# A fixed plan of expert blocks without branches, with two blocks interleaved, in a decoder layer on one core

## The chip, the cores and the metric

The kernel runs on one core of a Trainium2 chip. The metric is the device time of one execution in microseconds (us); less is better. The engines of a core work side by side: PE (TensorE, matrix products and transposes), DVE (VectorE), ACT (ScalarE) and POOL (GpSimd); SP (SyncE) issues most of the transfers, which 16 DMA engines carry out. Each engine has a program of its own and waits for the others by semaphores.

## The reference

One decoder layer on 2048 tokens of 1024 channels in fp32: two token mixers side by side (differential attention, and a causal convolution module), a gated merge, then a mixture of 32 experts and a gated per-layer embedding. The change is in the experts:

```python
g_idx = argmax(t @ w_rg + b_rg)                       # one of 4 groups
top_p, top_e = top_k(softmax(e_logits[g_idx]), 2)     # two of its 8 experts
...
def expert_block(args):
    xb, e = args
    hdn = jax.nn.silu(xb @ w1[e]) * (xb @ w3[e])      # [rows, 1024] @ [1024, 512], twice
    return hdn @ w2[e]                                # [rows, 512] @ [512, 1024]
...
h = h + moe
ple_gate = sigmoid(rmsnorm(h) @ w_ple_gate + b_ple_gate)
h = h + ple_gate * (p @ w_ple_proj)
```

Each token goes to two experts, so 4096 rows are spread over 32 experts, unevenly, and how many rows each has is known at run time only.

## The kernel before

Every fp32 operand is split into two parts of type fp32r: `split` (L92, L93) lets ACT copy the high part and DVE or POOL subtract it from the whole for the low part. A product is then three products, high by high, high by low and low by high (`mm3`, L97 to L99, or the lines L1144 to L1147).

The stages follow each other: the mixers and the merge, the routing (`route`, `pick`), the experts (`moe`), the per-layer embedding (`ple`). `pick` sorts the experts: expert 0 comes first, the others are ranked by their number of rows, and heavy and light ones alternate. It writes `idx` and `dst` (the rows of each block of 128, for gathering and for scattering) and `slots` (for each place in the order: the expert, its number of rows, its number of blocks).

An expert has 12 weight units of 128 x 1024 (512 KB): eight of w1 and w3 side by side, four of w2. `pull` issues a unit's load on SP's queue into a raw buffer (`eraw`, 9 of them) and splits it into `ewh` and `ewl` (15 pairs); units 2, 6 and 10 of an expert have their low part made by POOL, the others by DVE. Where the pulls stand in the program is a table written by hand (`PULLS`). The order of all five engines in the loop is the order of the code.

A block of up to 128 rows is gathered by POOL (`xs`), transposed by PE and split (`turned`: `tps`, `xt`); for each half f of the 512 hidden columns PE makes 24 products of 512 columns into `ups`, ACT and DVE make silu(a) * b (`gated`: `hd`), PE turns it (`turn`: `hps`, split into `hh`), and the products with w2 go to `yd` (`down`), are copied to `y` and scattered by POOL. A full block has 72 products. A block of at most 64 rows ("few", `both`, L1130 to L1133) puts its high and low parts side by side and needs 48, and DVE adds the two halves of each sum (`total`, L1136, L1137).

An expert's first block is always a full one. After half f = 0 of it all five engines load the expert's number of rows (L976) and branch: over 128 rows (L1030) the second block is computed inside the branch, as a full one if there are more than 192 rows (L1034) and as a short one otherwise, with nothing of the next expert's weights in between; `many` has further branches for a third block (L1005, L1007, L1009, L1010). Behind the branch the first block goes on.

The first queue behind the experts is that of `ple`: projections of the embedding for the first tiles (`pps`, AHEAD of them in front), then each tile's two expert rows (`ys`, from the scattered `Y`), the norm (`hn`), its transposes and the gate's products (`gps`).

## Time and profile before

| | |
|---|---|
| time, median of 3 runs (lowest, highest) | 2960.14 us (2957.19, 2967.8) |
| profiled execution, span from first to last instruction | 2960.1 us |
| PE busy | 2736.7 us (92% of the span) |
| PE weight loads, beside the products | 2282.7 us (77%) |
| DVE busy | 2041.7 us (69%) |
| ACT busy | 1474.9 us (50%) |
| POOL busy | 722.3 us (24%) |
| HBM read, written | 424.66 MB, 102.50 MB |

The span of the profiled execution is its own time; the runs beside it are timed without a profile. Shares of busy time are averages over stages that have different limits. Durations of matmuls overlap: PE takes one of 512 columns every 0.23 us at full clock, though each is shown with 0.39, so prices are read from starts, not from durations.

### The profile page before, as it was taken

To read this page: it belongs to the slowest core of one execution; us is meant where nothing else is said; L and a number is where in the kernel's file an instruction comes from. 1 tells how busy PE (TensorE), PEld (TensorE's weight loads), DVE (VectorE), ACT (ScalarE), POOL (GpSimd) and SP (SyncE) were. 2 spreads that over 40 slices of the span, in tenths; PEclk is the share of its full clock that TensorE was granted. 3 is DMA by queue.
4 is the path that set the end of the run, shared out by engine and by line. 5 is a ranking of instruction groups with operands and counts; after the bars stand their busy time and mean duration, and the time that the engine had idled before them with its cause. 6 is when DMAs were issued, how large, how long until landed. Compare 5 with 4: busy or idle time off the path is not lost. (4 is left out here: it accounts for less than half of the span.)

```text
span 2960.1 us, 40065 instructions
## 1 busy us (share of the span) xinstructions
PE 2736.7 (92%) x14078; PEld 2282.7 (77%) x14078; DVE 2041.7 (69%) x2860; ACT 1474.9 (50%) x2712; POOL 722.3 (24%) x463
## 2 busy tenths in 40 slices
PE   7999999999999999999999989898888989888988
PEld 5888877997778788787898867676666767666776
DVE  6995249995878888657567456666667777776564
ACT  4233352335766667544444345555455656565443
POOL 2021130123111000001101134544335444452122
PEclk9999999999999999999999989999999999999999
DMA  5134443235243331456556366777767776876371
GB/s 189 60 107 142 159 147 104 93 114 196 81 132 89 104 112 53 160 184 214 168 170 206 122 238 243 265 287 259 252 223 274 276 283 236 293 274 244 125 246 56
DMA packets 180220, 531.52 MB, mean 180 GB/s; under 512 B 19185, under 2 KB 48641, under 8 KB 179361
## 3 DMA queue, kind: packets, MB, share of 16 engines
q1 hardware_dynamic: 135536, 397.02, 39.9%
q0 software_dynamic: 25904, 92.45, 8.5%
q10 hardware_dynamic: 18432, 37.76, 3.4%
q8 instruction: 177, 2.90, 0.4%
q14 instruction: 171, 1.39, 0.1%
HBM read 424.66 MB, written 102.50 MB: 178 GB/s over the span
## 5 line engine op out<-in xcount | busy, mean ns | idle before, releaser
L93 DVE TENSOR_TENSOR ewl<-eraw,ewh 128x1024 fp32r<-128x1024 f32 x365 | 597.2, 1665 | 94.4 <-ACT ewh L92 88.5
L92 ACT ACTIVATE ewh<-eraw 128x1024 fp32r<-128x1024 f32 x464 | 474.1, 1065 | 54.0 <-PE mps L98 24.9
L387 DVE SCALAR_TENSOR_TENSOR co<-cb,pvt,co 128x1024 f32<-128x1024 f32 x240 | 313.6, 1345 | 1.6
L93 POOL TENSOR_TENSOR ewl<-eraw,ewh 128x1024 fp32r<-128x1024 f32 x99 | 253.8, 2563 | 185.4 <-ACT ewh L92 183.0
L1146 PE MATMUL ups<-ewh,xt 128*128 128x512 f32 x592 | 250.0, 422 | 40.3 <-issue 38.6
L1147 PE MATMUL ups<-ewl,xt 128*128 128x512 f32 x592 | 244.5, 413 | 0.9 <-DVE ewl L93 0.5
L97 PE MATMUL ps<-uh,wh 128*128 128x512 f32 x576 | 232.0, 405 | 4.4 <-ACT uh L92 4.4
L586 DVE TENSOR_REDUCE nm<-sc 128x1 f32<-128x512 f32 (+3 forms) x320 | 185.3, 606 | 66.1 <-PE sc L583 51.6
L98 PE MATMUL ps<-ul,wh 128*128 128x512 f32 x576 | 227.9, 397 | 1.1 <-POOL ul L93 1.1
L99 PE MATMUL ps<-uh,wl 128*128 128x512 f32 x576 | 227.2, 396 | 0.0
L1146 PEld LDWEIGHTS ups<-ewh,xt 128*128 128x128 f32 x592 | 119.0, 201 | 71.9 <-issue 46.0
L97 PE MATMUL ps<-wh,uh 128*128 128x384 f32 x512 | 173.0, 338 | 0.0
L99 PE MATMUL ps<-wh,ul 128*128 128x384 f32 x512 | 172.1, 336 | 0.0
L98 PE MATMUL ps<-wl,uh 128*128 128x384 f32 x512 | 172.0, 336 | 0.0
L1144 PE MATMUL ups<-ewh,xt 128*128 128x512 f32 x592 | 167.5, 406 | 3.7 <-issue 3.7
L97 PE MATMUL mps<-ewh,mh 128*128 128x256 f32 x512 | 150.3, 294 | 4.1 <-ACT mh L92 4.1
L403 POOL DMA_DIRECT2D G<-sg x64 | 35.1, 549 | 457.3 <-ACT sg L402 325.2
L98 PE MATMUL mps<-ewl,mh 128*128 128x256 f32 x512 | 145.8, 285 | 0.0
L99 PE MATMUL mps<-ewh,ml 128*128 128x256 f32 x512 | 145.2, 285 | 0.0
L1147 PEld LDWEIGHTS ups<-ewl,xt 128*128 128x128 f32 x592 | 119.3, 202 | 25.5 <-DVE ewl L93 1.0
L430 POOL TENSOR_TENSOR qn<-qk,qk_std 128x1024 f32<-128x1024 f32 x16 | 44.6, 2785 | 380.7 <-DVE qk_std L189 363.8
L1204 POOL DMA_INDIRECT Y<-y,dst x48 | 72.3, 1507 | 266.3 <-POOLq L1034 188.3
(340 smaller groups left out, 7238.5 us busy)
## 6 DMA issues: line engine op xcount, KB each, us to landing
eraw<-in_we SPq DMA_DIRECT2D x384, 512.0 KB, 7.3
G<-sg POOLq DMA_DIRECT2D x64, 256.0 KB, 2.7
eraw<-in_wac SPq DMA_DIRECT2D x32, 512.0 KB, 4.3
ga<-G SPq DMA_DIRECT2D x32, 512.0 KB, 5.1
eraw<-in_wo SPq DMA_DIRECT2D x32, 512.0 KB, 3.7
ys<-Y SPq DMA_DIRECT2D x32, 512.0 KB, 8.2
wraw<-in_wqkv SPq DMA_DIRECT2D x16, 768.0 KB, 4.2
wraw<-in_wg SPq DMA_DIRECT2D x20, 512.0 KB, 3.9
```

Of the source, the lines that this page charges most:

```text
L92: nc.scalar.activation(hi, x, AF.Copy)
L93: (lo_eng or nc.vector).tensor_tensor(lo, x, f32(hi), ALU.subtract)
L97: nc.tensor.matmul(ps, lh, rh, start=start, stop=False)
L98: nc.tensor.matmul(ps, lh, rl, start=False, stop=False)
L99: nc.tensor.matmul(ps, ll, rh, start=False, stop=stop)
L387: nc.vector.scalar_tensor_tensor(acc, cb[:, i : i + HALF], wi, acc, ALU.mult, ALU.add)
L430: nc.gpsimd.tensor_tensor(qn.rearrange("p t (s d) -> p t s d", d=HD), qk.rearrange("p t (s d) -> p t s d", d=HD), r.unsqueeze(3).to_broadc ...
L586: nc.vector.tensor_reduce(nm[:, qi, m, c : c + 1], sc[:, :w], AX.X, ALU.max, negate=True)
L1144: self.nc.tensor.matmul(ps, xt[1][:, k, :], wk[0], start=False, stop=k == NK - 1)
L1146: self.nc.tensor.matmul(ps, xt[0][:, k, :], wk[0], start=k == 0, stop=False)
L1147: self.nc.tensor.matmul(ps, xt[0][:, k, :], wk[1], start=False, stop=False)
L1204: nc.gpsimd.indirect_dma_start(out=self.Y[:, :], out_offset=bass.IndirectOffsetOnAxis(ap=dst[R], axis=0), in_=y[R], in_offset=None)
```

## The change

PLAN gives each rank a fixed list of blocks, full (128 rows) or short (64): 30 full and 19 short ones for the 32 experts. SLOTS puts heavy and light ranks in turn. The loop has no branch on a number any more. A heavy expert's two blocks share each pair of weight units (`U(a, f, g)`, `U(b, f, g)`); a light expert's last transposes and products are held back and placed behind the next expert's first unit (`held`, `release`). `pull` is placed by a small planner (`did`, `small`): it counts what PE and DVE have been given so far, 1.17 us for a split, and issues the next split as long as DVE's count is at most SLACK = 1.5 us ahead of PE's. All splits go to DVE. The buffers: 8 raw ones instead of 9, 14 pairs instead of 15, three `eu` and three `ed` banks (before: two `eu` for the first block and two `ev` for the second, two `ed`), `xt` twice and a short `fx`. `pick` computes in addition which experts have more rows than planned; `rest()`, behind the loop, redoes these block by block if there are any. In `ple` five projections stand ahead instead of six.

```diff
-AHEAD = 6
+AHEAD = 5
-MOE_W = (9, 15)
-POOL_UNITS = (2, 6, 10)
-PULLS = (1, 1, 1, 2, 3, 2, 2)
+MOE_W = (8, 14)
+FULL, PART = P, FEW
+PLAN = [[FULL, FULL], [FULL, FULL, PART]] + [[FULL, FULL]] * 3 + [[FULL, PART]] * 11 + [[FULL]] * 9 + [[PART]] * 7
+SLOTS = [PLAN[s // 2 if s % 2 == 0 else NE - 1 - s // 2] for s in range(NE)]
+UNIT_US = 1.17
+SLACK = 1.5
...
-                W[e].append(self.unit(src[c], nc.gpsimd if c in POOL_UNITS else nc.vector, after))
+            W[e].append(self.unit(src[c], None, after))
+            pulled += 1
+            dve = max(dve, pe) + UNIT_US
+
+        def did(us):
+            nonlocal pe
+            pe += us
+            while dve <= pe + SLACK and pulled < 12 * NE + 12 and (pulled < MOE_W[1] or pulled - MOE_W[1] in last):
+                pull()
...
+        def U(j, f, g):
+            while pulled <= 12 * j.e + 4 * f + 2 * g + 1:
+                pull()
...
+            if g == 1:
+                j.h[f] = self.gated(j.u[f], j.few)
+                small(1.1 if j.few else 0.4)
+            did(1.82 if j.few else 2.72)
...
+            for i, g in enumerate(groups):
+                nxt = groups[i + 1] if i + 1 < len(groups) else [None]
+                a = g[0]
+                for j in g:
+                    X(j)
+                U(a, 0, 0)
+                release()
+                if len(g) == 2:
+                    b = g[1]
+                    U(b, 0, 0)
+                    release()
+                    U(a, 0, 1)
+                    U(b, 0, 1)
+                    U(a, 1, 0)
+                    T(a, 0)
+                    U(b, 1, 0)
+                    T(b, 0)
+                    U(a, 1, 1)
+                    U(b, 1, 1)
+                    DN(a, 0, 0)
+                    T(a, 1)
+                    DN(b, 0, 0)
+                    X(nxt[0])
+                    T(b, 1)
+                    DN(a, 1, 0)
+                    DN(a, 0, 1)
+                    DN(b, 1, 0)
+                    DN(b, 0, 1)
+                    DN(a, 1, 1)
+                    DN(b, 1, 1)
+                else:
+                    U(a, 0, 1)
+                    release()
+                    if nxt[0] and not (a.few and nxt[0].few):
+                        X(nxt[0])
+                    U(a, 1, 0)
+                    T(a, 0)
+                    U(a, 1, 1)
+                    DN(a, 0, 0)
+                    DN(a, 0, 1)
+                    for j in nxt:
+                        X(j)
+                    held = [lambda a=a: T(a, 1), lambda a=a: (DN(a, 1, 0), DN(a, 1, 1))]
+            release(2)
+            while pulled < 12 * NE + 12:
+                pull()
+            self.rest()
...
+    def rest(self):
+        some = nc.values_load(self.over[0:1, 0:1], engines=engines, min_val=0, max_val=NBLK)
+        with tc.If(some > 0):
```

The first place is PE's program in the first expert, before the change: the end of the first block's half f = 0 (`ups_16327`), the load of the number of rows, two branches, and the start of the second block (`ups_16392`), which begins with units 0 and 1 again.

```order
L1144 MATMUL ups_16327<-ewh_16265,xt_16219 128x512 x2
L1144 MATMUL ups_16327<-ewh_16271,xt_16219 128x512 x2
L976 TENSOR_LOAD slots_11526
L1030 COMPARE_AND_BRANCH
L1034 COMPARE_AND_BRANCH
L1146 MATMUL ups_16392<-ewh_16253,xt_16234 128x512
L1147 MATMUL ups_16392<-ewl_16254,xt_16234 128x512
L1146 MATMUL ups_16392<-ewh_16253,xt_16234 128x512
```

The same place after the change; `ups_16384` is the first block's sum, `ups_16397` the second's, and `ewh_16281`, `ewh_16304` and `ewh_16310` are the high parts of units 0, 1 and 2.

```order
L1265 MATMUL ups_16384<-ewh_16281,xt_16262 128x512 x2
L1265 MATMUL ups_16384<-ewh_16304,xt_16262 128x512 x2
L1262 MATMUL ups_16397<-ewh_16281,xt_16285 128x512
L1263 MATMUL ups_16397<-ewl_16282,xt_16285 128x512
...
L1265 MATMUL ups_16397<-ewh_16281,xt_16285 128x512 x2
L1265 MATMUL ups_16397<-ewh_16304,xt_16285 128x512 x2
L1262 MATMUL ups_16384<-ewh_16310,xt_16262 128x512
```

The second block takes its products with units 0 and 1 right behind the first block's, before unit 2 is read, and the load of the number and the branches are gone.

The second place is DVE's program inside such a branch, before: the product `hd` and the low part `hh` of the second block's two halves, and no split (`ewl`) between them.

```order
L1030 COMPARE_AND_BRANCH
L1034 COMPARE_AND_BRANCH
L1170 TENSOR_TENSOR hd_16417<-hd_16417,ups_16392 128x256
L93 TENSOR_TENSOR hh_16391<-hps_16433,hh_16391 128x256
L1170 TENSOR_TENSOR hd_16450<-hd_16450,ups_16420 128x256
L93 TENSOR_TENSOR hh_16475<-hps_16476,hh_16475 128x256
L1005 COMPARE_AND_BRANCH
```

The same place after the change, from the first block's second `hd` (`hd_16496`) to both blocks' second `hh` (`hh_16551`, `hh_16584`); `hd_16523` is the second block's, `xt_16570` a tile of 64 rows of the next expert.

```order
L1279 TENSOR_TENSOR hd_16496<-hd_16496,ups_16440 128x256
L92 TENSOR_TENSOR ewl_16502<-eraw_16499,ewh_16501 128x1024
L92 TENSOR_TENSOR ewl_16508<-eraw_16505,ewh_16507 128x1024
L1279 TENSOR_TENSOR hd_16523<-hd_16523,ups_16459 128x256
L92 TENSOR_TENSOR ewl_16529<-eraw_16526,ewh_16528 128x1024
L92 TENSOR_TENSOR ewl_16535<-eraw_16532,ewh_16534 128x1024
L92 TENSOR_TENSOR ewl_16548<-eraw_16545,ewh_16547 128x1024
L92 TENSOR_TENSOR hh_16551<-hps_16552,hh_16551 128x256
L92 TENSOR_TENSOR ewl_16567<-eraw_16564,ewh_16566 128x1024
L92 TENSOR_TENSOR xt_16570<-tps_16571,xt_16570 128x8x64
L92 TENSOR_TENSOR hh_16584<-hps_16585,hh_16584 128x256
```

Splits of the next expert now stand between `hd` and `hh`, three of them ahead of `hh_16551`. In a short block of a light expert it reads as follows: the sum (`ft`), `hd`, a split, the tile of the next expert, a split, `hh`.

```order
L1254 TENSOR_TENSOR ft_16706<-ft_16706,ups_16682 64x512
L1279 TENSOR_TENSOR hd_16705<-hd_16705,ft_16706 64x256
L92 TENSOR_TENSOR ewl_16714<-eraw_16711,ewh_16713 128x1024
L92 TENSOR_TENSOR xt_16717<-tps_16718,xt_16717 128x4x128
L92 TENSOR_TENSOR xt_16717<-tps_16725,xt_16717 128x4x128
L92 TENSOR_TENSOR ewl_16746<-eraw_16743,ewh_16745 128x1024
L92 TENSOR_TENSOR hh_16749<-hps_16750,hh_16749 128x2x64
```

Before the change a first block was never short, so this row of operations did not stand there.

## Rows read from the trace of the kernel before

**Rows 1.** Busy time in three stretches of the span (microseconds from its start): everything up to the experts, the expert stage, the last stage. Columns: stretch, its length, busy time and instructions (x) of PE, PE's weight loads, DVE, ACT and POOL, mean granted clock of PE as a share of full speed, share of the DMA engines, GB/s.

```profile
0.00:1727.80 1727.80, 1647.46 (x9274) 1427.23 (x9274) 1234.70 (x2081) 813.02 (x1749) 244.97 (x201) 0.98 0.41 136
1727.80:2711.00 983.20, 870.79 (x3812) 676.88 (x3812) 670.85 (x632) 554.10 (x803) 425.84 (x229) 0.94 0.73 262
2711.00:2960.10 249.10, 218.46 (x992) 178.63 (x992) 136.10 (x148) 107.76 (x162) 51.46 (x35) 0.95 0.44 154
```

**Rows 2.** The expert stage grouped by line, engine, operation, tile and shape. Columns: group and count (x), busy us, mean ns of one | idle time of the engine just before them and what ended it. L1144 multiplies the low part of a full block's rows, L1130 is the first product of each sum of a short block, L1111 transposes a tile of gathered rows.

```profile
L1144 PE MATMUL ups<-ewh,xt 128*128 128x512 f32 x592 | 167.5, 406 | 3.7 <-issue 3.7
...
L1111 PE MATMUL tps<-cst,xs 128*128 128x128 f32 x368 | 47.9, 273 | 0.0
...
L1130 PE MATMUL ups<-ewh,xt 128*128 128x512 f32 x24 | 11.7, 489 | 33.6 <-issue 32.1 <-POOL xt L81 1.5
```

**Rows 3.** PE's instructions in four places of the expert stage: start, duration, engine, line, operation, tiles, shape, count. First the transposes of one half of the hidden rows (`hps`) and the product behind them, then the transposes of a tile of rows (`tps`) and the product behind them, then two rows 12 products apart in a full block, and two in a short one.

```profile
1769.51 0.38 PE L1177 MATMUL hps<-cst,hd 128*128 128x128 f32 x2
1769.65 0.48 PE L97 MATMUL yd<-ewh,hh 128*128 128x512 f32 x1
...
1771.12 1.03 PE L1111 MATMUL tps<-cst,xs 128*128 128x128 f32 x8
1771.91 0.48 PE L97 MATMUL yd<-ewh,hh 128*128 128x512 f32 x1
...
1803.39 1.07 PE L1144 MATMUL ups<-ewh,xt 128*128 128x512 f32 x4
...
1806.11 1.07 PE L1144 MATMUL ups<-ewh,xt 128*128 128x512 f32 x4
...
1827.17 0.40 PE L1133 MATMUL ups<-ewh,xt 128*128 128x512 f32 x1
...
1829.94 0.40 PE L1133 MATMUL ups<-ewh,xt 128*128 128x512 f32 x1
```

**Rows 4.** What PE waited for in the expert stage, by line: instruction that waited, what ended the wait ("issue": nothing that the profile shows; DVEq: DVE's sequencer), us in total, times, longest.

```profile
PE ups L1146 <- issue: 38.6, 16, 3.3
PE ups L1130 <- issue: 32.1, 11, 3.5
PE hps L1177 <- DVEq L1030: 14.5, 10, 2.7
...
PE hps L1177 <- DVE hd L1170: 4.5, 2, 3.9
```

**Rows 5.** PE around two branches, in order of time; in brackets the idle time before an instruction and what ended it.

```profile
1765.12 0.41 PE L1177 MATMUL hps<-cst,hd 128*128 128x128 f32 x2 [1.44 <-PEq L1005]
...
1767.22 1.08 PE L1144 MATMUL ups<-ewh,xt 128*128 128x512 f32 x4
...
1779.27 1.07 PE L1144 MATMUL ups<-ewh,xt 128*128 128x512 f32 x4
1782.84 0.79 PE L1146 MATMUL ups<-ewh,xt 128*128 128x512 f32 x1 [2.50 <-issue]
1783.43 0.63 PE L1147 MATMUL ups<-ewl,xt 128*128 128x512 f32 x1
...
1785.98 0.39 PE L1147 MATMUL ups<-ewl,xt 128*128 128x512 f32 x1
```

**Rows 6.** Splits and sums on DVE: all subtractions of the stage that DVE made, in one group (columns as in group 2), then single ones from the timeline, with the one of POOL that overlaps the last, the two subtractions of a tile of rows, and the product (`hd`) of a short block's half.

```profile
L93 DVE TENSOR_TENSOR ewl<-eraw,ewh 128x1024 fp32r<-128x1024 f32 x294 | 508.6, 1765 | 48.1 <-ACT ewh L92 42.3
...
1832.25 0.42 DVE L1170 TENSOR_TENSOR hd<-hd,g 64x256 f32<-64x256 f32 x1 [0.48 <-ACT hd L1169]
...
1845.77 1.22 DVE L93 TENSOR_TENSOR ewl<-eraw,ewh 128x1024 fp32r<-128x1024 f32 x1
...
1846.77 2.50 POOL L93 TENSOR_TENSOR ewl<-eraw,ewh 128x1024 fp32r<-128x1024 f32 x1 [4.47 <-ACT ewh L92]
...
1847.20 1.29 DVE L93 TENSOR_TENSOR xt<-tps,xt 128x512 fp32r<-128x512 f32 x2 [0.21 <-ACT xt L92]
...
1848.64 1.72 DVE L93 TENSOR_TENSOR ewl<-eraw,ewh 128x1024 fp32r<-128x1024 f32 x1
```

**Rows 7.** Four engines' rows around a product `hd` in the queue of DVE (timeline, in order of time).

```profile
1739.62 9.34 DVE L93 TENSOR_TENSOR ewl<-eraw,ewh 128x1024 fp32r<-128x1024 f32 x5 [1.47 <-ACT ewh L92]
...
1744.23 0.36 ACT L1169 ACTIVATE hd<-ups 128x256 f32<-128x256 f32 x1
...
1748.89 0.41 DVE L1170 TENSOR_TENSOR hd<-hd,ups 128x256 f32<-128x256 f32 x1
...
1749.35 0.69 PE L1177 MATMUL hps<-cst,hd 128*128 128x128 f32 x2 [3.92 <-DVE hd L1170]
```

**Rows 8.** The weight loads: the group of DMA issues (KB each, median us from issue to landing), one stretch of 10 us (columns as in group 1), and what the queue that issues the loads waited for in the expert stage (total, times, longest).

```profile
eraw<-in_we SPq DMA_DIRECT2D x384, 512.0 KB, 7.3
...
1790.00:1800.00 10.00, 10.00 (x55) 8.41 (x54) 8.59 (x11) 8.51 (x13) 4.26 (x5) 1.00 1.03 409
...
SPq L1084 <- DVE ewl L93: 432.9, 219, 31.1
```

**Rows 9.** PE at the end of the expert stage and the start of the last: the last product of the last expert, the first projection, the first transposes of a tile that has the experts' rows in it.

```profile
2710.57 0.39 PE L99 MATMUL yd<-ewh,hh 128*128 128x512 f32 x1
2712.58 0.50 PE L97 MATMUL pps<-ewh 128*128 128x512 f32 x1 [1.62 <-ACT y L1202]
...
2734.09 1.06 PE L1111 MATMUL tps<-cst,hn 128*128 128x128 f32 x8 [0.54 <-DVE hn L1276]
```

More of the change, by code (lines that the diff above doesn't have):

```diff
@@ L141, in keep @@
         self.slots = cp.tile([1, 3, NE], I32, name="slots")
+        self.over = cp.tile([1, 1], I32, name="over")
         self.xp = self.ctx.enter_context(self.tc.tile_pool(name="xp", bufs=2, reuse_waits="tile"))
@@ new lines, in rows, with X @@
+        def rows(k):
+            if k < len(jobs) and jobs[k].x is None:
+                j = jobs[k]
+                j.x = self.xp.tile([P, D], F32, name="xs", tag="xs")[j.R]
+                self.gather(col(self.idx, j.e, j.b)[j.R], j.x)
+        def X(j):
+            if j is None or j.done:
+                return
+            j.done = True
+            j.xt = self.turned(j.x, j.few)
+            rows(j.k + 2)
+            small(0.64 if j.few else 1.28)
+            did(0.5 if j.few else 0.87)
@@ new lines, in U @@
+        def U(j, f, g):
+            while pulled <= 12 * j.e + 4 * f + 2 * g + 1:
+                pull()
+            w = W[j.e]
+            if g == 0:
+                j.u[f] = self.eu.tile([P, 512], F32, name="ups", tag="eu")
+            if j.few:
+                self.products_few(w, j.xt, f, j.u[f], g)
+            else:
+                for i in range(2):
+                    self.products(w, j.xt, f, j.u[f], g, i)
+            if j.ends:
+                for c in range(2):
+                    last[12 * j.e + 4 * f + 2 * g + c] = True
+            if g == 1:
+                j.h[f] = self.gated(j.u[f], j.few)
+                small(1.1 if j.few else 0.4)
+            did(1.82 if j.few else 2.72)
@@ new lines, in T, with DN @@
+        def T(j, f):
+            j.ht[f] = self.turn(j.h[f], j.few)
+            small(0.4)
+            did(0.2)
+        def DN(j, f, n):
+            while pulled <= 12 * j.e + 8 + 2 * f + 1:
+                pull()
+            if f == 0:
+                j.yd[n] = self.ed.tile([P, 512], F32, name="yd", tag="ed")
+            self.down(W[j.e], j.yd[n], f, j.ht[f], j.few, n)
+            if f and n == 0:
+                j.y = self.ep.tile([P, D], F32, name="y", tag="y")
+            if f:
+                yn = j.y[j.R, n * 512 : (n + 1) * 512]
+                if j.few:
+                    self.total(yn, j.yd[n])
+                    small(0.68)
+                else:
+                    nc.scalar.copy(yn, j.yd[n])
+            if n and j.ends:
+                for c in range(2):
+                    last[12 * j.e + 8 + 2 * f + c] = True
+            did(0.91 if j.few else 1.36)
+            if f and n:
+                self.scatter(j.y, col(self.dst, j.e, j.b), j.R)
@@ new lines, in moe @@
+        jobs, groups = [], []
+        for e, plan in enumerate(SLOTS):
+            new = []
+            for b, n in enumerate(plan):
+                new.append(Job(len(jobs), e, b, n == PART, False))
+                jobs.append(new[-1])
+            new = [new[:2], new[2:]] if len(new) > 2 else [new]
+            new[-1][-1].ends = True
+            groups += new
+        for j, x in zip(jobs, self.first):
+            j.x = x
+        self.ctx.enter_context(tc.manual_schedule(engines={ET.SP}))
@@ L1075, in column, with scatter @@
+    def scatter(self, y, dst, R):
+        self.nc.gpsimd.indirect_dma_start(
+            out=self.Y[:, :], out_offset=bass.IndirectOffsetOnAxis(ap=dst[R], axis=0), in_=y[R], in_offset=None
+        )
     def column(self, t, b, tag):
@@ L1171, in gated, with turn @@
         return hd
-    def turn(self, hd, ht, few=False):
+    def turn(self, hd, few):
         n = FEW if few else P
+        ht = self.ep.tile([P, 4, P], F32R, name="hh", tag="hh", bufs=4)
         ps = self.et.tile([P, 512], F32, name="hps", tag="et")[:, : 2 * n]
```

278 lines of the change are left out of this document (107 added, 171 removed).

## The prediction

> **What bounds the kernel now.** I read the stage windows first. The expert stage takes 983.2 us of the 2960.1, and in it the tensor engine (PE) is busy 870.8 us, the vector engine (DVE) 670.9, the scalar engine (ACT) 554.1, and the DMA engines have a share of 0.73 [rows 1]. PE comes nearest to its window, but 112.4 us of it are idle and its mean granted clock is 0.94. The change touches the stage before only by a few small operations and the stage behind by its start, so the sum is made over the middle window.
>
> How much of 983.2 is work? The grouped rows give the blocks: 592 matmuls of the low part at 16 per full block are 37 full blocks, 24 first products at two per short block are 12 short ones, and 368 transposes at 8 per tile are 46 transposed tiles [rows 2]. The dense stretches give the price. Two rows 12 products apart start at 1803.39 and 1806.11, so a product of a full block costs 0.227 us; in a short block 12 products run from 1827.17 to 1829.94, 0.231 each; from a tile's transposes to the next product pass 0.79 us, from those of a half 0.14 [rows 3]. At full clock without a wait the stage would be 37 x 72 x 0.2267 = 603.9, plus 12 x 48 x 0.2308 = 132.9, plus 46 x 0.79 = 36.3, plus 2 x 49 transposes of halves x 0.14 = 13.7: **786.9 us**. The other 196 us are waits and what follows them.
>
> The waits of PE name them. Of the 112 us, 38.6 (16 times) and 32.1 (11 times) stand before the first product behind a branch and wait for nothing that the profile shows; 14.5 us (10 times) wait for the branch L1030 on DVE's sequencer [rows 4]. The timeline shows one: products end at 1780.3, the next starts at 1782.84, and from there to 1785.98 seven take 3.14 us instead of 1.59, which is the lower of the two clock levels; behind a gap of 1.44 us at 1765 two transposes and eight products take 2.10 us, the full clock [rows 5]. So a branch costs a gap, and a gap of 2.5 us costs 1.5 us more.
>
> **What the change removes.** (1) All run-time branches of the loop, with the 85 us of waits above and the low clock behind them. (2) Seven first blocks become short: 30 full and 19 short ones instead of 37 and 12. Routing worked out from the reference's inputs gives the seven lightest experts 43 to 28 rows, and every expert fits the plan, so the loop at the end is not entered. The new work: 30 x 72 x 0.2267 = 489.7, 19 x 48 x 0.2308 = 210.5, 28 full transposed tiles at 0.79 = 22.1, 19 tiles of 64 rows, which no row shows, between 0.4 (half as many columns) and 0.79, taken as 0.5 = 9.5, and 13.7: **745.5 us**, 41 below the same sum of before.
>
> **What it adds.** (3) All splits go to DVE. A subtraction on DVE took 1.22 us at 1845.77 with nothing on GpSimd (POOL), 1.72 at 1848.64 beside one of POOL's, and 1.765 in the mean of 294 [rows 6]. With POOL's gone I take 1.22: 392 x 1.22 = 478, the 162 us that DVE now has besides (670.9 less 508.6), and 18 for the 28 sums of seven more short blocks (0.65 each, half of the pair at 1847.20): 658 us, hidden behind PE's 745.5. The upper bound is 1.765.
>
> (4) Order on DVE. The instructions behind an interleaved pair stand as `hd`, three `ewl`, `hh`. PE needs that `hh` after 1.36 + 0.14 + 1.36 + 0.5 = 3.4 us (six products, transposes, six products, a tile's transposes); DVE and ACT need 0.8 for `hd` (ACT 0.36, DVE 0.41 [rows 7]), 3 x 1.22 and 0.4: 4.9, so PE waits 1.5. With a short second block the sums come first (from the half's last product at 1829.94 to the end of `hd` at 1832.67 [rows 3, 6], less the product, 2.3) and two `ewl` follow: 5.1 against 3.2, 1.9. The 5 and 11 such pairs give 28 us. In a light expert, a full block has 7.4 (0.8, two `ewl`, 1.29 for `xt`, two `ewl`, 0.4) against 0.79 + 2.72 + 0.14 + 2.72 = 6.4, a short one 2.3 + 1.22 + 1.29 + 1.22 + 0.4 = 6.4 against 4.6: 9 x 1.0 + 7 x 1.8 = 22. Together **50 us**; bounds are 0 (the splits are done before `hd` is ready) and 130 (two more splits of 1.22 in each of the 32 places). Gaps of 1 to 2 us lie between the 1.44 that kept the clock and the 2.50 that lost it [rows 5]; at 1.5 us for each of 16 they cost 0 to 24; as most are near the lower one, I take **5**.
>
> (5) Loads. A unit of 512 KB lands 7.3 us after its issue, and the 983.2 us moved 262 GB/s x 983.2 = 258 MB; a window of 10 us at 409 GB/s shows what the engines can move, so the transfers need at least 630 us [rows 8]. The queue spent 432.9 us waiting for DVE to free raw buffers [rows 8], so loads follow splits. With 8 raw and 14 split buffers instead of 9 and 15, and a share of about 0.73 x 983 / 818 = 0.88, some loads will be late where a short expert uses 12 units in 11 us: **10 us** (0 to 40). The first expert starts on loads that are still landing: **8** (0 to 16, two landings).
>
> (6) Held products: a light expert's last transposes and products stand behind the next expert's first unit. That takes the wait for its last `hh` off PE and costs no instruction; the cover is 2.72 us of products.
>
> (7) Behind the loop there is one branch on a loaded number, then the last stage. Now PE starts its projections 1.62 us late at 2712.58, and the first transposes behind the scattered rows come at 2734.09, 23.5 us after the last product [rows 9]. With 5 projections ahead instead of 6, 2.7 us of products (12 at 0.23) leave that stretch and come later; the branch (about 3.5, a gap as at 1782.84 with its low clock) lies beside scatter and loads, and buffers for `ys` are fewer. Ahead of the stage, `pick` gets five small operations on DVE in front of the row lists (at most 0.4 each, the price of `hd` [rows 7]: 2 us), while PE projects. **+6** together (0 to 15).
>
> Sum: 745.5 + 50 + 5 + 10 + 8 = 818.5 for the stage, 164.7 less than 983.2; with +6 the kernel takes 2960.1 - 158.7 = 2801, and I put it at **2803 us**. The profiled execution had the span 2960.1, and the median of the runs is 2960.14, so nothing has to be converted.
>
> **The strongest argument against it.** DVE takes its instructions in order. At 1739.62 it began five `ewl` that lasted 9.34 us; ACT had finished its part of `hd` at 1744.59, DVE's part came only at 1748.89, and PE had waited 3.92 us for it and went on at half clock [rows 7]. The change puts more splits ahead of such small operations, and a split waits for its load.
> [...]
>
> **Rivals.**
> *A load in front of a small operation* (slower). If once per expert a small operation stands behind a split whose load was just issued, PE waits a whole landing: 32 x 7.3 = 234, and 1.5 each for the clock, 48. The stage is 745.5 + 282 + 18 = 1045, the kernel about **3028**. It decides from (983.2 - 6 - 745.5 - 18) / 32 = 6.7 us per expert on. For it: [rows 7], and the share of 0.88. Against it: up to 8 loads are in flight, as the queue issues as soon as a raw buffer is free, and 8 units last PE more than 7 us.
> *DVE or the loads become the bound.* At 1.765 per split without POOL as well, DVE needs 692 + 162 + 18 = 872 and 18 at the start: 983 falls to 890, the kernel **2873**; loads late by 40 to 100 us give 2835 to 2895. DVE decides from 1.63 per split ((818.5 - 180) / 392). Against it: 1.22 at 1845.77.
> *Nothing waits.* PE runs dense: 745.5 and 8, the kernel about **2736** to 2765.
> *The plan doesn't hold.* If an expert had more rows than planned, the loop behind the stage would redo it with one raw buffer: 12 landings and splits, 12 x (7.3 + 2.3) = 115 us a block. One such block gives about **2916**, two are slower than before. The 37 and 12 blocks of the trace are the plan's 32 first, 16 second and one third; that seven first ones are light comes from the inputs.
>
> **Chances.** My forecast, 2765 to 2845, has 0.66; nothing waits 0.10; DVE or loads 0.15; a load in front 0.05; the plan 0.04. The range is **2750 to 2880**: it takes in the forecast's 0.66, about 0.06 of the case below and 0.09 of the bound by DVE or loads. A measurement of this kernel tells about 0.5% (15 us) from no change. Faster by more than that: 0.92 (the first three, with one in three of the plan's); the same 0.03, slower 0.05.
>
> **What the profile of the changed kernel would show.** (1) No waits for "issue" or a branch in the expert stage, and a clock above 0.94. (2) 480 matmuls of the low part, 38 first products of short blocks. (3) No split on POOL, and a mean near 1.22 on DVE; near 1.7 it was not POOL. (4) PE's waits for `hh`, for `hd` or for the transposes' buffers, 1 to 2 us each, some 30 times, 50 us in all. (5) A share of 0.85 to 0.9; waits of ACT for loads and of PE for `ewh` or `ewl` under 20 us. (6) No wait before the held products. (7) 22 to 30 us from the last expert product to the first transposes of the last stage. The prediction is wrong if DVE's splits stay at 1.7, if PE waits for splits that wait for loads, or if the low clock stays although the branches are gone.

## The result, and the profile after

The changed kernel takes 2869.68 us in the median of four runs (2867.16 to 2875.22), the kernel before 2959.24 beside it: a ratio of 0.9685, 95% interval 0.9663 to 0.9708. It is 90 us faster. The range of 2750 to 2880 holds that, the forecast of 2803 was 67 us too low. The profiled execution has a span of 2865.1 us.

The same three stretches as in [rows 1], cut at the first expert product and at the last:

```profile
0.00:1718.40 1718.40, 1641.93 (x9274) 1423.62 (x9276) 1240.21 (x2118) 812.94 (x1748) 241.78 (x200) 0.98 0.42 137
1718.40:2608.90 890.50, 813.69 (x3646) 618.75 (x3644) 624.72 (x744) 563.98 (x804) 112.14 (x94) 0.96 0.80 278
2608.90:2865.10 256.20, 220.69 (x992) 178.67 (x992) 124.58 (x145) 93.95 (x149) 43.81 (x17) 0.95 0.44 150
```

The expert stage went from 983.2 to 890.5 us, the last stage from 249.1 to 256.2, and the stage began 9.4 us earlier (the start varies by up to 7 us over the profiles shown here, so not all of that is the change). PE is idle for 76.8 us of the stage instead of 112.4, and its granted clock is 0.96 instead of 0.94. What it waits for is now something else than in [rows 4]:

```profile
PE tps L1239 <- DVE hh L92: 25.6, 9, 3.7
PE hps L1287 <- DVE xt L92: 20.5, 14, 2.6
PE hps L1287 <- DVE hh L92: 11.5, 6, 3.5
PE hps L1287 <- DVE hd L1279: 6.5, 2, 6.0
PE ups L1247 <- DVE xt L92: 3.7, 9, 2.3
PE ups L1263 <- DVE ewl L92: 2.6, 3, 1.1
...
PE ups L1262 <- ACT ewh L91: 1.0, 1, 1.0
```

No wait for a branch is left. The waits for split weights (`ewl`, `ewh`) are small; five sixths of the time (64 us) go to transposes (`tps`, `hps`) that wait for a small operation of DVE. The grouped rows of the stage show the new blocks (480 / 16 = 30 full, 38 / 2 = 19 short) and the new price of a split:

```profile
L92 DVE TENSOR_TENSOR ewl<-eraw,ewh 128x1024 fp32r<-128x1024 f32 x395 | 467.0, 1221 | 135.7 <-ACT ewh L91 135.0
...
L1265 PE MATMUL ups<-ewh,xt 128*128 128x512 f32 x480 | 129.9, 393 | 0.0
...
L1247 PE MATMUL ups<-ewh,xt 128*128 128x512 f32 x38 | 17.7, 467 | 3.9 <-DVE xt L92 3.7
```

One pair's tail, from the timeline of all engines (start, duration, engine, line, operation, count, idle time before it):

```profile
2412.04 0.38 PE L1287 MATMUL hps<-cst,hd 128*128 128x128 f32 x2
...
2412.56 1.99 ACT L91 ACTIVATE ewh<-eraw 128x1024 fp32r<-128x1024 f32 x2
2412.68 0.42 DVE L1279 TENSOR_TENSOR hd<-hd,ft 64x256 f32<-64x256 f32 x1 [0.48 <-ACT hd L1278]
...
2413.20 0.60 PE L1239 MATMUL tps<-cst,xs 128*128 128x128 f32 x4
2413.63 2.36 DVE L92 TENSOR_TENSOR ewl<-eraw,ewh 128x1024 fp32r<-128x1024 f32 x2 [0.53 <-ACT ewh L91]
...
2415.91 0.42 DVE L92 TENSOR_TENSOR hh<-hps,hh 128x256 fp32r<-128x256 f32 x1
...
2416.38 0.66 PE L1239 MATMUL tps<-cst,xs 128*128 128x128 f32 x4 [2.59 <-DVE hh L92]
...
2418.08 0.63 PE L98 MATMUL yd<-ewh,hh 128*128 128x512 f32 x1
...
2418.51 0.63 PE L96 MATMUL yd<-ewh,hh 128*128 128x512 f32 x1
...
2421.00 0.40 PE L96 MATMUL yd<-ewh,hh 128*128 128x512 f32 x1
```

The first block's `hps` are in their bank at 2412.4. ACT first makes two `ewh`, DVE an `hd` and two `ewl`, and only at 2415.91 comes the `hh` that reads that bank. The transposes of the next expert's tile need the bank (there are two), so PE stands still for 2.59 us; then products come 0.43 us apart until 2421.0, the lower clock level (granted clock 0.53 from 2417.3 to 2420.6, 1.00 from 2421 to 2424, where they are 0.23 us apart).

To compare kernels, the stage is taken apart from all starts on PE: its idle time, the excess of "slow products" (0.33 to 0.70 us behind the one before with no wait between, less 0.227), and the rest, which is work. Where the limits are drawn moves single entries by up to 3 us. Of the 33.4 us of slow products in the changed kernel, 6.0 are single starts 0.33 to 0.35 us behind the one before, which stand at full clock too (2.9 us before the change). Each ratio is to the kernel before, timed beside that run. The last column is each ratio less the changed kernel's, times 2959 us; by the intervals of the two ratios it is uncertain by some 14 us for e1 to e4 and 10 us for the others.

| kernel | median, us | ratio (95%) | stage | idle | slow products | rest | against the changed kernel |
|---|---|---|---|---|---|---|---|
| before | 2959.2 | | 983.1 | 112.3 | 51.6 | 819.2 | +93 |
| changed | 2869.7 | 0.9685 (0.9663-0.9708) | 890.5 | 76.6 | 33.4 | 780.5 | |
| e1_fill | 2864.9 | 0.9690 (0.9648-0.9731) | 886.4 | 48.5 | 19.0 | 819.0 | +1 |
| e2_hush | 2830.6 | 0.9564 (0.9525-0.9604) | 847.7 | 51.4 | 18.3 | 778.0 | -36 |
| e3_et3 | 2844.5 | 0.9613 (0.9574-0.9653) | 868.3 | 63.5 | 27.1 | 777.8 | -21 |
| e4_cover | 2832.2 | 0.9572 (0.9532-0.9613) | 853.7 | 50.2 | 23.8 | 779.7 | -33 |
| e5_pool | 2928.0 | 0.9898 (0.9873-0.9923) | 950.3 | 115.2 | 53.5 | 781.6 | +63 |
| e6_full | 2878.4 | 0.9731 (0.9706-0.9756) | 898.8 | 58.7 | 22.6 | 817.5 | +14 |
| e7_seq | 2857.7 | 0.9666 (0.9643-0.9690) | 881.9 | 71.2 | 26.4 | 784.3 | -6 |
| e8_noheld | 2938.7 | 0.9938 (0.9915-0.9962) | 959.6 | 112.5 | 62.9 | 784.2 | +75 |
| c1_both | 2913.0 | 0.9838 (0.9813-0.9863) | 922.5 | 89.9 | 46.9 | 785.7 | +45 |
| c3_seqquiet | 3252.3 | 1.0974 (1.0939-1.1008) | 1261.0 | 268.3 | 163.6 | 829.2 | +381 |
| d1_quiet_light | 2834.8 | 0.9578 (0.9549-0.9606) | 854.3 | 53.7 | 20.6 | 780.0 | -32 |
| d2_quiet_et3 | 2808.6 | 0.9494 (0.9470-0.9518) | 830.9 | 38.8 | 16.2 | 775.8 | -57 |

### The profile page after: what moved, and what is told of

The parts are those of the page before. It is cut to its first block, busy times and chain, and to the rows that moved or that the text cites. A ratio compares the mean times of both kernels' runs of the same rounds, so it can differ in the third digit from the quotient of the medians.

```text
span 2865.1 us, 38604 instructions
## 1 busy us (share of the span) xinstructions
PE 2676.3 (93%) x13910; PEld 2221.0 (78%) x13911; DVE 1989.5 (69%) x3006; ACT 1470.9 (51%) x2700; POOL 397.7 (14%) x311
## 5 line engine op out<-in xcount | busy, mean ns | idle before, releaser
L92 DVE TENSOR_TENSOR ewl<-eraw,ewh 128x1024 fp32r<-128x1024 f32 x464 | 551.2, 1221 | 180.9 <-ACT ewh L91 179.8
L98 PE MATMUL ps<-uh,wl 128*128 128x512 f32 x576 | 227.3, 396 | 0.0
L1262 PE MATMUL ups<-ewh,xt 128*128 128x512 f32 x480 | 196.1, 409 | 1.0 <-ACT ewh L91 1.0
L1263 PE MATMUL ups<-ewl,xt 128*128 128x512 f32 x480 | 190.4, 397 | 2.6 <-DVE ewl L92 2.6
L98 PE MATMUL ps<-wh,ul 128*128 128x384 f32 x512 | 172.1, 336 | 0.0
L98 PE MATMUL mps<-ewh,ml 128*128 128x256 f32 x512 | 144.8, 284 | 0.0
L96 PEld LDWEIGHTS ps<-uh,wh 128*128 128x128 f32 x576 | 109.0, 190 | 32.4 <-ACT uh L91 4.9
L97 PEld LDWEIGHTS ps<-ul,wh 128*128 128x128 f32 x576 | 108.9, 189 | 30.1 <-POOL ul L92 2.0
L1265 PE MATMUL ups<-ewh,xt 128*128 128x512 f32 x480 | 129.9, 393 | 0.0
L582 PE MATMUL sc<-Kt,Qt 128*128 128x512 f32 (+2 forms) x320 | 125.7, 399 | 3.4 <-ACT pr L572 2.8
L98 PEld LDWEIGHTS ps<-uh,wl 128*128 128x128 f32 x576 | 108.4, 188 | 26.2
L91 ACT ACTIVATE ah<-tp 128x512 fp32r<-128x512 f32 x144 | 82.6, 603 | 81.0 <-PE tp L632 68.9
L92 DVE TENSOR_TENSOR wl<-wraw,wh 128x1024 fp32r<-128x1024 f32 (+1 forms) x50 | 79.1, 1584 | 64.5 <-ACT wh L91 59.0
```

The source lines that it names most:

```text
L91: nc.scalar.activation(hi, x, AF.Copy)
L92: (lo_eng or nc.vector).tensor_tensor(lo, x, f32(hi), ALU.subtract)
L96: nc.tensor.matmul(ps, lh, rh, start=start, stop=False)
L97: nc.tensor.matmul(ps, lh, rl, start=False, stop=False)
L98: nc.tensor.matmul(ps, ll, rh, start=False, stop=stop)
L582: nc.tensor.matmul(sc[:, :n], Qt[:, 2 * m, qs], ks, start=True, stop=False)
```

## Experiments

All are edits of the changed kernel; the label behind a heading is that of the table. The first four take on the tail of a pair, its last transposes and products.

**Filling the wait with work** (e1_fill)

```diff
                     DN(b, 0, 0)
+                    fill(a)
                     X(nxt[0])
```

> Edit: in each of the 16 interleaved pairs, 11 extra products of 128x512 (of operands that lie ready, into a bank whose sum is used nowhere) stand in front of the next expert's transposes, where the tensor engine waits about 2.6 us for the vector engine. 176 products at 0.227 us are 40 us more work. Theory A (the wait is idle time, and the low clock behind it comes from the idle time): the waits there shrink from 2.6 us to about 0.3, the products behind them run at 0.23 us instead of 0.43, and the kernel gets faster by 16 x 1.3 = 20 us, although it does more. Rival 1 (the low clock does not come from these gaps): the filled waits cost nothing and give nothing, the time stays within 5 us, the slow products remain. Rival 2 (the engine is not really free there): 40 us slower.

`fill` makes 11 products of 128x512 into a bank that nobody reads. PE in one such place (timeline):

```profile
2417.82 2.69 PE L1111 MATMUL fill<-ewh,hh 128*128 128x512 f32 x11
2420.34 1.33 PE L1246 MATMUL tps<-cst,xs 128*128 128x128 f32 x8
2422.35 0.33 PE L1294 MATMUL hps<-cst,hd 64*128 64x64 f32 x2 [0.68 <-DVE xt L93]
...
2422.95 0.39 PE L98 MATMUL yd<-ewl,hh 128*128 128x512 f32 x1
2423.18 0.39 PE L99 MATMUL yd<-ewh,hh 128*128 128x512 f32 x1
```

Work rose by 38.5 us, idle time fell by 28.1 and slow products by 14.4, and the ratio is that of the changed kernel within its interval. Neither a gain of 20 us nor a loss of 40: the place is idle time, and the low clock behind it goes when PE has something to do there (behind the 0.68 us the pitch is 0.23). By the time alone rival 1 would fit, but it would have left the slow products; rival 2 would have added 40 us. The expected gain was too high because not all 16 places waited 2.6 us: 37 us of idle time and 20 of slow products were to go, 28 and 14 did, about as much as the fill costs.

**No splits in the tail of a pair** (e2_hush)

```diff
-            while dve <= pe + SLACK and pulled < ...
+            while not quiet and dve <= pe + SLACK and pulled < ...
...
+                    quiet = True
                     U(b, 1, 1)
...
                     T(b, 1)
+                    quiet = False
```

> Edit: the planner places no splits between a pair's last w1/w3 products and the second block's last transposes; they come later. Theory A (splits ahead of hh in the queues of the vector and scalar engines make the tensor engine wait there): the heavy places' waits fall from 2.6-3.7 us to under 0.8, 16 x 2.2 = 35 us, and the slow products behind them, 15 to 25 us, go as well: 50 to 60 us faster than the changed kernel, about 2815. Rival 1 (the waits come from the two banks for transposes, or from the chain hd-transposes-hh itself): the waits stay over 2 us, the time within 10 us. Rival 2 (splits that come later make products wait for their weights instead): waits for ewl or ewh rise from 5 us to over 30, the gain is under 20 us.

Waits of PE in the expert stage:

```profile
PE hps L1289 <- DVE xt L92: 28.7, 24, 3.0
...
PE ups L1265 <- DVE ewl L92: 2.8, 3, 1.1
...
PE tps L1241 <- DVE hh L92: 2.7, 3, 0.9
```

The 25.6 us of `tps` waiting for `hh` became 2.7, slow products fell by 15, and the splits were not late. So the splits ahead of `hh` made PE wait. The gain is 36 us instead of 50 to 60, since a wait of 0.7 to 1.0 us stays in the 11 pairs with a short second block, in six of them now for `xt` and its bank.

**Three banks for transposes** (e3_et3)

```diff
-        self.eu = ctx.enter_context(tc.tile_pool(name="eu", bufs=3, ...))
-        self.et = ctx.enter_context(tc.tile_pool(name="et", bufs=2, ...))
+        self.eu = ctx.enter_context(tc.tile_pool(name="eu", bufs=2, ...))
+        self.et = ctx.enter_context(tc.tile_pool(name="et", bufs=3, ...))
```

> Edit: three banks for transposes instead of two, two for the first sums instead of three. The profile names tps and hps as what waits for hh: a bank of transposes that has not been read. Theory A (the order on the vector engine): the wait moves to the first product that needs hh itself (yd), and shrinks only by the transposes that now stand in front of it, 0.5 to 0.8 us each: 8 to 15 us less of waits, the time 5 to 30 us lower, as some gaps fall below what keeps the clock. Rival 1 (the banks): the waits of the heavy places go, 50 us faster. A cost of its own would be waits of ups for hd, as there are two banks for sums only.

```profile
PE hps L1287 <- DVE hh L92: 21.7, 9, 3.3
PE yd L1247 <- DVE hh L92: 12.9, 8, 1.9
PE yd L98 <- DVE hh L92: 8.9, 14, 1.2
PE ups L1262 <- DVE hd L1279: 7.7, 1, 7.7
```

The wait moves, to the products that need `hh` themselves (21.8 us) and in nine places still to a bank; 13 us of idle time and 21 us of the time are gone. The bank is the place where the late `hh` shows first; it is a part of the cause, worth 21 us, not the whole of it. That is theory A; the cost of its own came as one wait of 7.7 us for `hd`, in place of one of 6.0 that stood in the first expert anyway.

**More products in front of the wait** (e4_cover)

```diff
                     DN(b, 0, 0)
-                    X(nxt[0])
                     T(b, 1)
-                    DN(a, 1, 0)
                     DN(a, 0, 1)
+                    DN(a, 1, 0)
+                    X(nxt[0])
                     DN(b, 1, 0)
```

> Edit: in the interleaved pairs both last transposes come first, then the first block's second half of the columns for f = 0 (six products), then its products that need hh; the next expert's transposes come behind. The splits stay where the planner puts them. Theory A: hh comes when it came, but 1.36 us of products more stand in front of it and the transposes of a tile less: the waits fall from 2.6 to about 1.5 us, which keeps the full clock, so 16 x (1.1 + 1.3) = 38 us faster. Rival 1 (any wait of over 1 us costs the clock): only 16 x 1.1 = 18 us. Rival 2 (the wait is for the bank alone): it disappears, 60 us faster.

The gain is 33 us against 38 expected, without a change to the splits. That the two are so close is luck: theory A had 18 us of waits and 21 of slow products, and it was 26 and 10. The waits for `hh` of the pairs with a short second block are 0.6 us each now, not 1.5 (9.0 us, 15 times, at L98), in four pairs with 1.0 us for `hd` ahead of it. No slow products follow them; of the waits at L98 only the one of 1.16 us at the end of the stage has some behind it.

**Undoing one part at a time.** Splits back on POOL (e5_pool):

```diff
-            W[e].append(self.unit(src[c], None, after))
+            W[e].append(self.unit(src[c], nc.gpsimd if c in (2, 6, 10) else nc.vector, after))
```

> Edit: units 2, 6 and 10 of each expert have their low part made by GpSimd again, as in the kernel before; the rest is the changed kernel. Theory A (two engines that subtract at the same time slow each other): the mean of a split on the vector engine goes from 1.22 back to about 1.7 us, its 294 splits cost 500 us against 467, the small operations wait as long as now or longer behind them, and the time is 0 to 20 us above the changed kernel. Rival 1 (the price of 1.22 has another cause, such as loads or the scalar engine): the mean stays near 1.22, the vector engine has 120 us less to do, fewer splits stand ahead of small operations, and the kernel is 10 to 30 us faster.

```profile
L92 DVE TENSOR_TENSOR ewl<-eraw,ewh 128x1024 fp32r<-128x1024 f32 x295 | 472.7, 1630 | 162.9 <-ACT ewh L91 159.6 <-PE ups L1248 2.6
L92 POOL TENSOR_TENSOR ewl<-eraw,ewh 128x1024 fp32r<-128x1024 f32 x99 | 249.2, 2518 | 272.8 <-ACT ewh L91 250.2 <-issue 11.0 <-DVE ewl L92 10.9
```

DVE's split goes from 1.221 to 1.630 us in the mean, so 295 splits take 473 us where 395 took 467: POOL's quarter of the work frees nothing on DVE. That is theory A. Its price was far too low: 63 us instead of 0 to 20. Single waits for `hh` reach 5.3 us, idle time grows by 39 us and slow products by 20; the largest growth is of a short block's first product, which waits for `xt` (23.8 us in all, 3.7 in the changed kernel).

The mean hides two kinds of split. In the timeline:

```profile
2191.09 2.58 POOL L92 TENSOR_TENSOR ewl<-eraw,ewh 128x1024 fp32r<-128x1024 f32 x1
2191.34 1.28 DVE L92 TENSOR_TENSOR xt<-tps,xt 128x512 fp32r<-128x512 f32 x2
...
2192.87 1.88 DVE L92 TENSOR_TENSOR ewl<-eraw,ewh 128x1024 fp32r<-128x1024 f32 x1 [0.25 <-ACT ewh L91]
```

POOL's split ends at 2193.67, DVE's at 2194.75, 1.08 us later. So it is with all: of DVE's 295 splits 213 took 1.21 to 1.26 us, and the other 82 ended 1.08 to 1.09 us behind the end of a POOL split, however long before it they had begun (up to 4.4 us in all). In the kernel before it was 197 and 97 of 294, the 1.72 of [rows 6] among the 97. So in these two traces a split on DVE either took what it takes alone or ended 1.08 to 1.09 us behind a split of POOL; none was slowed by a share. It is the same in e5 with `hd` of a short block, which has both inputs in SBUF too: 32 of 38 took 0.42 us, the other six (up to 2.25 us) ended 0.28 to 0.29 us behind a split of POOL. `xt` and `hh`, which read one of their two inputs from PSUM, were not held up: each of the 94 `xt` before the change, 61 of them beside a split of POOL, took 0.68 to 0.69 us, and in e5 the means of `xt` and of the two sizes of `hh` were 0.683, 0.415 and 0.282 us, against 0.684, 0.418 and 0.283 in the changed kernel.

Full first blocks for the light experts (e6_full; `[[PART]] * 7` becomes `[[FULL]] * 7`):

> Edit: the seven lightest experts have a full block instead of a short one. By products alone it is 7 x (72 x 0.227 - 48 x 0.231) = 37 us more work and 2 for the transposes. Theory A (the waits depend on what covers the chain on the vector engine): a short light block waits 2.3 to 2.6 us with a low clock behind it, a full one 0.8 us, so about 7 x 3 = 20 us come back: 19 us slower than the changed kernel. Rival 1 (work alone counts): 39 us slower. Rival 2 (the tensor engine is not the bound): within 5 us.

The rest rose by 37.0 us, as worked out, and 18 us of idle time and 11 of slow products came back: 8.3 us more in the stage, 14 by the ratios, where theory A said 19. A shorter block also covers less; most of the 37 us that it saves go into waits and the low clock behind them.

A heavy expert's blocks one after the other (e7_seq):

```diff
-            new = [new[:2], new[2:]] if len(new) > 2 else [new]
+            new = [[j] for j in new]
```

> Edit: a heavy expert's blocks run one after the other, each like a light expert's (last products held behind the next block's first unit), instead of interleaved by pairs of units. Theory A (interleaving spreads the freeing of split buffers over both blocks): the first block frees nothing, the second frees twelve buffers in 11 to 16 us and the next light expert wants its twelve units right behind, so products wait for ewl and ewh, about 5 us for each of 16 pairs: 50 to 90 us slower than the changed kernel. Rival 1 (the held products are the better cover and the buffers suffice): the 16 waits of 2.6 us and their low clock go, 40 us faster. Rival 2: within 10 us, one wait for the other.

Within the intervals the time is that of the changed kernel, and the stage 8.6 us shorter: rival 2, and theory A falls. Waits for `ewl` and `ewh` are 11.1 us in all instead of 50 to 90. Interleaving by pairs of units is not what makes this change faster; the waits of the pairs' tails go and others take their place.

Without holding a light expert's last products (e8_noheld):

```diff
-                    held = [lambda a=a: T(a, 1), lambda a=a: (DN(a, 1, 0), DN(a, 1, 1))]
+                    T(a, 1)
+                    DN(a, 1, 0)
+                    DN(a, 1, 1)
```

> Edit: a light expert's last transposes and products stand right behind its other products, not behind the next expert's first unit. Theory A: hh comes 4 to 6 us after the last w1/w3 product, and 1.4 to 2.7 us of products and a tile's transposes cover it: a wait of 2 to 3 us and 1.6 us of low clock in each of 16 places, 50 to 70 us slower than the changed kernel. Rival 1 (the cover of the products and transposes is enough): within 10 us.

75 us slower, theory A: idle time rose by 36 us and slow products by 30. The places are `yd` waiting for `hh`, on ACT mostly 1.3 to 1.8 us and then on DVE 1.0 to 1.3 us, in most of them with the low clock behind the two together. This run is also the nearest to a price for step (6).

**Putting the mends together.** Both mends of the tail (c1_both), and also no splits in a light expert from its first sum to the transposes of its first half (`quiet = True` ahead of `U(a, 0, 1)`, `False` behind `T(a, 0)`):

> Edit: the quiet stretch without splits and the changed order of the pair's last products together, and no splits in a light expert between its first sum and the transposes of its first half. Theory A (each wait is one of the order on the vector and scalar engines): the pairs' waits go (37 us with 15 to 20 of low clock), and those of the light experts (hps for xt, 20 us with some 10 of low clock) fall to under 8: about 2790 to 2800, with waits of 20 to 30 us in the whole stage. Rival 1 (the two edits mend the same wait and the light experts' wait is of the banks): the time stays at that of the better of the two, 2825 to 2835. Rival 2 (splits that are put off come too late): waits for ewl and ewh of 20 us or more.

The timeline of all engines, from the middle of a light expert:

```profile
2405.42 0.38 ACT L1282 ACTIVATE hd<-ups 128x256 f32<-128x256 f32 x1 [2.30 <-PE ups L1269]
2405.70 3.89 ACT L91 ACTIVATE ewh<-eraw 128x1024 fp32r<-128x1024 f32 x4
...
2406.78 4.63 DVE L92 TENSOR_TENSOR ewl<-eraw,ewh 128x1024 fp32r<-128x1024 f32 x4 [0.53 <-ACT ewh L91]
...
2406.80 0.49 PE L96 MATMUL yd<-ewh,hh 128*128 128x512 f32 x1 [1.42 <-ACT ewh L91]
...
2413.58 0.62 PE L1266 MATMUL ups<-ewh,xt 128*128 128x512 f32 x1 [1.63 <-ACT ewh L91]
...
2414.84 0.79 PE L1267 MATMUL ups<-ewl,xt 128*128 128x512 f32 x1 [0.64 <-DVE ewl L92]
2415.43 0.63 PE L1266 MATMUL ups<-ewh,xt 128*128 128x512 f32 x1
```

Slower than the changed kernel by 45 us, rival 2. ACT waits 2.30 us with nothing to do, since no split may be issued; the four that the next products need come all at once behind `hd`, and PE waits for each. Waits for `ewh` and `ewl` are 57.3 us in the stage instead of 4.4. Here is the other side of the same balance: splits too far ahead delay small operations, splits too late delay products. The run does not tell how much of it the light experts' stretch makes alone.

Blocks one after the other, each with that quiet stretch (c3_seqquiet):

> Edit: a heavy expert's blocks one after the other as in the run without interleaving, with no splits between each block's first sum and the transposes of its first half. Theory A: the waits of hps for xt (27.6 us there) fall to under 8 and the low clock with them, 25 to 35 us faster than that run, about 2825 to 2835; if it beats the interleaved kernel with the quiet stretches, interleaving is not needed for the cover. Rival: six splits in a row then stand ahead of the last hh, and the wait moves to yd: the time stays within 10 us of 2858.

3252 us, slower than before the change, which neither theory had: the waits for `ewh` and `ewl` are 241 us in the stage. The largest:

```profile
PE ups L1264 <- ACT ewh L91: 81.5, 57, 1.9
PE ups L1265 <- DVE ewl L92: 52.8, 74, 1.1
PE yd L96 <- ACT ewh L91: 43.3, 28, 2.8
```

The quiet tail of the pairs and three banks for transposes (d2_quiet_et3):

> Edit: the quiet stretch in the pairs (as in the run with it alone) and three banks for transposes, two for the first sums; the instructions' order is that of the run with the quiet stretch alone. What is left there is 28.7 us of hps waiting for xt, which no instruction needs: it is the bank. Theory A (that wait is the ring of two banks): it goes, a shorter wait for hh takes its place in the light experts, 15 to 20 us less of waits and low clock: about 2810 to 2815. Rival 1 (the hh behind the same splits is as late as the bank): within 6 us of 2831. Rival 2 (two banks for sums make ups wait for hd): slower than 2831.

```profile
PE yd L1249 <- DVE hh L92: 12.9, 8, 1.9
...
PE yd L98 <- DVE hh L92: 6.1, 10, 1.2
```

2808.6 us, 57 us faster than the changed kernel and 150 faster than before: the best version. The 28.7 us for the bank are gone, and products wait 19 us for `hh` in their place (4 with the quiet tail alone). Theory A held.

The quiet tail, and a light expert's transposes moved ahead of the next tile's with one short quiet stretch (d1_quiet_light):

> Edit: the quiet stretch in the pairs, and in a light expert the transposes of its first half before those of the next expert's tile, with no splits issued between (a stretch of one unit's products, where the run with both stretches had one of three steps). Theory A: the wait of hps for xt (28.7 us) becomes one of the next tile's transposes for hh, 0.4 to 0.9 us each, 12 to 20 us less: about 2812 to 2820, with waits for ewl and ewh under 10 us. Rival 1 (splits put off once more come late, as in the run with both stretches): waits for ewh and ewl of 30 us or more, and a time of 2860 to 2910.

No better than the quiet tail alone: the wait for the bank became 15.4 us of the tile's transposes for `hh`, and the waits for `hd` rose from 5.3 to 14.7 us. Theory A named the wait that came, but not the one for `hd`; waits for splits stayed at 7.4 us, so rival 1 fell as well.

## Why the prediction came out as it did

**The direction and the mechanism were right, the size was not.** The forecast was that branch waits go and that smaller waits take their place where `hh` stands behind splits. The 85 us of [rows 4] are gone, and of the 76.6 us that are left 57.6 are in `tps` and `hps` rows that wait for `hh` or `xt`. So idle time fell by 36 us only; slow products fell by 18, and work by 39: that is the stage's 93 us. The sum was 67 us too low in total, and 72 of it lie in the stage (890.5 against 818.5). The time lies outside the 2765 to 2845 of the forecast; the range of 2750 to 2880 holds it because it took in a part of two rivals. That the time is near the 2873 of "DVE or the loads become the bound" is chance: DVE was busy for 70% of the stage.

**The base was taken as a sum and not as a difference: 35 us.** Step (2) worked out 786.9 us before and 745.5 after, and called all 196 us that were left of 983.2 "waits and what follows them". Idle time and slow products are 164 of these. The stage before has 819.2 us of work and the one after 780.5, so both sums are 32 to 35 us too low: a product behind transposes starts the next one 0.31 us later, not 0.23 (1769.65 [rows 3], the next at 1769.96), the product in front of a short block's `hps` lasts 0.32 to 0.33 us from start to start where no wait comes between (23 times before the change) and so does the one in front of a short tile's `tps` (19 times after it), and a tile of 64 rows took 0.64 us instead of 0.5. The difference was nearly right, 39 against 41. Had the step taken its 41 from 819, this error would have cancelled.

**The clock: 28 us.** Step (4) took 5 us for the low clock, between 0 and 24, because the waits were to be 1.0 to 1.9 us. They were 2.3 to 3.7 in 17 places, and slow products cost 33.4 us, more than the upper bound (27 without the 6.0 that stand at full clock too; these belong to the base). e1 showed that this loss goes with the idle time (33.4 us became 19.0). The step also read too much from two gaps, 1.44 us that kept the clock and 2.50 that lost it. The same trace has a gap of 1.76 us that lost it (0.43 us from product to product) and one of 2.63 that kept it (0.23):

```profile
2046.62 0.49 PE L1146 MATMUL ups<-ewh,xt 128*128 128x512 f32 x1 [2.63 <-issue]
...
2047.17 0.39 PE L1146 MATMUL ups<-ewh,xt 128*128 128x512 f32 x1
2047.41 0.40 PE L1147 MATMUL ups<-ewl,xt 128*128 128x512 f32 x1
...
2167.18 0.50 PE L1146 MATMUL ups<-ewh,xt 128*128 128x512 f32 x1 [1.76 <-issue]
...
2169.06 0.63 PE L1146 MATMUL ups<-ewh,xt 128*128 128x512 f32 x1
2169.49 0.63 PE L1147 MATMUL ups<-ewl,xt 128*128 128x512 f32 x1
```

**The waits: 9 us.** Forecast 50 + 10 + 8, measured 76.6. The 11 pairs with a short second block waited 2.6 us (seven) or 3.5 to 3.7 (four) instead of 1.9, the five others 0 to 1.7 instead of 1.5: 37 us together instead of 28. Two terms were missing: ACT's queue, whose `ewh` came late for DVE's `ewl` (0.53 us at 2413.63) and stands ahead of `hh` there too, and the ring of two banks, by which the next tile's second transposes wait too, so that 0.4 us of the counted cover lay behind the wait. The light experts came out near the forecast: mostly 2.3 to 2.6 us instead of 1.8 with a short block, 0.8 and 0.2 instead of 1.0 with a full one. Late loads, put at 10 us, cost less (4.4 us of waits for split weights); the DMA share is 0.80.

The three add up to 72. **Outside the stage** the last one is 7.1 us longer (forecast +6 with the small operations), though not by the mechanism named: the first transposes come 19 us after the last product instead of 23.5 [rows 9], and PE's idle time behind them is longer (35.5 us in the whole last stage instead of 30.6), of which the waits for `hn` are the smaller part (13.5 us instead of 11.8); where the rest comes from stays open. The stage's start came 9.4 us earlier, where the forecast had some 2 us later; most of that is within what the start varies by.

**Other steps.** (3) 1.22 per split was right (1.221), and e5 confirms its reason, more sharply than the step had it: the 82 splits that took longer were not slower by a share, each ended 1.08 to 1.09 us behind a split of POOL. Its worth was not seen: the step asked only whether DVE would become the bound and priced POOL's removal at nothing. Put back, POOL costs 63 us, because a split that has to wait makes every small operation behind it later. (6) was priced at nothing too; e8 gives it 75 us. (2) at 41 us of work is worth 14 when undone alone. (4)'s interleaving is worth nothing by itself (e7). These don't add up to 90: each is measured with the others in place. What the branches alone cost was not tried by itself; that their waits went is read from the rows, and how much of the 90 us is theirs is not shown.

**The rivals.** A load in front of a small operation did not occur: ACT waited 6.4 us for loads in the whole stage. DVE did not become the bound. The plan held.

## What to carry to other kernels

DVE has two jobs here, bulk work that may come any time and small operations that PE waits for, and it made an `hh` only behind the two splits that stood ahead of it (2415.91, with PE idle for 2.59 us). What costs is not its load (70% busy) but what stands directly in front of the small ones; a quiet stretch ahead of each, or other work for the waiting engine, is worth more than less work (36 and 33 us here, against 14), and a stretch that is too long makes the bulk late, which costs more (c1 and c3, slower by 45 and 381 us). Take the difference of two sums made in the same way, not a sum against a measured time, and price a helper on a second engine by what it does to the first (POOL's quarter of the splits cost 63 us): look at each operation beside it, as a mean can hide that some wait and the others don't.

## What the runs showed of the chip

Over the expert stages of the fourteen traces, PE's waits that stood alone (no other in the 7 us before and the 4 us behind) were followed by the two clock levels (0.23 and 0.43 us from product to product) like this. Behind each of 178 of 0.6 to 1.75 us at most 0.3 us was lost; of 110 between 1.75 and 3.0 us 71 were followed by the lower level, and of 47 longer ones 46. In between, the length alone did not decide: in the changed kernel two waits of 2.59 us, at 2309.56 and 2579.16, were followed by the full clock (0.23 us from product to product), two of 2.59, at 2362.23 and 2416.38, by seven and nine slow products. In the changed kernel, 12 of the 17 waits of 2.3 to 3.7 us were followed by 4 to 13 slow products, 1.0 to 2.7 us lost each time, and five by none. Two short waits close to each other could cost it too: 1.63 and 0.64 us in c1, at 2413.58 and 2414.84, with 2.5 us lost behind them.

DVE's subtraction of 128 x 1024 with both inputs in SBUF took 1.21 to 1.26 us each of the 395 times in the changed kernel. In the two kernels that split on POOL as well it took longer 179 times, and each time it ended 1.08 to 1.09 us behind the end of one of POOL's. POOL's indirect transfers, nearly all of its 94 operations in the stage after the change, left it at 1.22.
